# Small software scratch, a third staging and a fourth split buffer for weights, and other places and orders at the entrance of a channel mixer

## The chip, the cores and the metric

The kernel runs on one core of one Trainium2 chip. The metric is the device time of one execution in microseconds (us); the time before is the median of three runs. Engines: PE is TensorE, DVE VectorE, ACT ScalarE, POOL GpSimd, SP SyncE, which here issues all transfers.

## The reference

A two-layer encoder trunk over 512 tokens of width 1024 in float32:

```
for layer in range(2):
    hn = rms_norm(x, norm_mix_pre[layer])
    m  = retention_na_mixer(hn, ...) if layer == 0 else ssd_mixer(hn, ...)
    x  = x + rms_norm(m, norm_mix_post[layer])
    f  = conv_geglu_ffn(rms_norm(x, norm_ffn_pre[layer]), ...)
    x  = x + rms_norm(f, norm_ffn_post[layer])
```

The first mixer joins retention heads and two-dimensional neighbourhood attention. The second, a state-space mixer, projects to z, x, B, C and dt, convolves x, B and C over five tokens, scans in both directions in chunks of 128, adds a skip, gates with silu(z), normalises in four groups and projects with w_out. The channel mixer is

```
u = conv3(hn @ w_up) + b;  gate, val = split(u);  (gelu(gate) * val) @ w_down
```

with an inner width of 2816 (22 blocks of 128).

## The kernel before

Each float32 operand of a large product is split into a high part (rounded to the matmul's format) and a low part (the rest), and each product is three matmuls: high by high, high by low, low by high (`mm3`, L83 to L88). `split` (L79 to L82) makes a pair: ScalarE copies the high part, VectorE subtracts to get the low part.

Weights come in units of 512 KB. `wunit` (L55) loads one into a staging tile `wst`, of which there are 2, and splits it into `whi` and `wlo`, of which there are 3 each; or, with `parts`, into four tiles of half the width given by the caller. These weight splits have a raised priority of 60. The activations lie in `xh` and `xl`, eight blocks of 128 features by 512 tokens.

`norm(t)` makes the normalised tile `xs` of 128 tokens; `turn(t)` (L134) transposes it with eight small matmuls into `pt` and splits that into `xh` and `xl` without a raised priority. `post_norm` (L168) adds a sublayer's normalised output to x, read from tiles `mg`.

The order of instructions on every engine, the queues of transfers included, is set by a planner: it walks a simulated time with a cost model, takes among the instructions that are ready the one that stands first in the program (a raised priority moves it ahead by that many instructions), and gives tiles their slots. It then puts in the waits. Every engine runs its list in order. Tiles come from pools. The pools of a stage are stacked behind those of the whole kernel; when a stage ends, the next one's pools come to lie on the same bytes, and they have to wait for the users of what lay there.

The second token mixer, `mixer1`, ends with group 3 of its heads: projections t6 and t7 with Silu into tiles `z` (L689, L692), `head` (decay matrices `e`, `ds` from rows `pb` that are broadcast from DRAM, L736), `inter` (`pi`, `ti`), `pair` (`py`, `y`, `yh`, `yl`). Its last output weights are four units: two in `whi` and `wlo`, two in memory that group 3 no longer needs (tiles `wo`). Then, for four tiles of 128 tokens and two halves of the width, `out_tile` makes `m` from the product and the sum of the other groups, which is kept in x (L828). Since x itself had been saved to DRAM as `xd`, it is loaded back at once (L829, on SyncE's queue); a square of `m`, the scaled tile `mg`, `post_norm` and `norm` follow.

`ffn` (L214) is the channel mixer. Its pool `ffn_h` holds 22 tiles `hh` and 22 `hl`; a second pool of it, `ffn_c`, holds the conv weights `cwt`, whose transfer is the first that `ffn` issues. Its first four units (up-projection, two blocks of gate and value) are loaded ahead: the first and second go to `whi` and `wlo`, the third and fourth to two `hh` and two `hl` each. Their products are made first for tokens 0 to 255 (column half c = 0), with the turns of token tiles 2 and 3 in between (`E.flush()`), then for tokens 256 to 511 (c = 1). Then come the convolutions and blocks 2 to 21, and the down-projection, `down_tm`.

All of it is preceded by a reserved scratch at the start of each SBUF partition, by default of 16384 bytes, for transfers whose descriptors are made in software.

Of the kernel before, what the change touches and what calls it, by code (L numbers as in the profile page):

```python
# [7 lines left out]
F32 = mybir.dt.float32  # L8
R32 = mybir.dt.float32r
# [6 lines left out]
P = 128  # L16
S = 512
# [5 lines left out]
NF = FFN // P  # L23


class Env:


    def __init__(self, ctx, tc):
        self.tc, self.nc = tc, tc.nc  # L30
        nc = self.nc
        pool = lambda name, bufs, **kw: ctx.enter_context(tc.tile_pool(name=name, bufs=bufs, **kw))
        self.const = pool("const", 1)
        self.res = pool("res", 1)
        self.wst = pool("wst", 2)
        self.whi = pool("whi", 3)
        self.wlo = pool("wlo", 3)
        self.gain = pool("gain", 2)
        self.tmp = pool("tmp", 7)
        self.small = pool("small", 6)  # L40
        pool("pad", 1).tile([P, 32], F32, name="pad")
        self.mm = pool("mm", 4, space=PSUM)
        self.px = pool("px", 4, space=PSUM)
        self.dram = pool("dram", 1, space=DRAM)


        head = self.const.tile([P, 96 + P], F32, name="head")
        self.ident, self.mhalf = head[:, 96:], head[:, 0:1]
        make_identity(nc, self.ident)
        nc.vector.memset(self.mhalf, -0.5)  # L50
        self.x = self.res.tile([P, NT, D], F32, name="x")
        self.xh = self.res.tile([P, KD, S], R32, name="xh")
        self.xl = self.res.tile([P, KD, S], R32, name="xl")
        self.late, self.xs = [], {}
# [79 lines left out]
    def turn(self, t):  # L134

        nc = self.nc
        for h, xs in enumerate(self.xs[t]):
            pt = self.px.tile([P, 4, P], F32, name="pt", tag="px")
            for j in range(4):
                nc.tensor.transpose(pt[:, j], xs[:, j * P:(j + 1) * P], self.ident)  # L140
            o = (slice(None), slice(h * 4, h * 4 + 4), slice(t * P, (t + 1) * P))
            self.split(self.xh[o], self.xl[o], pt)

    def post_half(self, st, t, n, ps, g_post, eng=None, m=None):

# [38 lines left out]
def down_tm(E, batches, w_dram, act, g_post, done, extra):  # L184

    st, ps = {}, {}
    nk = w_dram.shape[1] * 2
    k0 = [0, 0]  # L190
    for b, parts in enumerate(batches):
        last = b == len(batches) - 1
        ws = [(n, k0[n] + 2 * i, w_dram[n, k0[n] // 2 + i]) for n, u in parts for i in range(u)]
        ws = [(n, k, E.wunit(w, extra(i) if last else None)) for i, (n, k, w) in enumerate(ws)]
        for n, u in parts:
            k0[n] += 2 * u
        for t in range(NT):
            tt = slice(t * P, (t + 1) * P)
            for n, k1, w in ws:
                if k1 == 0:  # L200
                    late = len(ps) >= NT and last and len(parts) > 1 and t == 0
                    ps[n, t] = (E.px if late else E.mm).tile([P, 512], F32, name="mm", tag="px" if late else "mm")
                for i in range(2):
                    ah, al = act(k1 + i)
                    E.mm3(ps[n, t], ah[:, tt], al[:, tt], *w[i], k1 + i == 0, k1 + i == nk - 1)
                if k1 + 2 == nk:
                    E.post_half(st, t, n, ps[n, t], g_post)
            if last:
                E.finish(DOWN[t], st, done)
    E.late += [lambda s=s: E.finish(s, st, done) for s in LATE]  # L210


def ffn(E, w_up, cw, w_down, g_post_row, done):

    nc, tc = E.nc, E.tc
    with ExitStack() as ctx:
        hp = ctx.enter_context(tc.tile_pool(name="ffn_h", bufs=NF))
        cp = ctx.enter_context(tc.tile_pool(name="ffn_c", bufs=1))
        cwt = cp.tile([P, 2, NF, 4], F32, name="cwt")
        nc.sync.dma_start(cwt, cw)  # L220
        hs = []

        def conv(ps, s, f):
            w = lambda i: cwt[:, s, f, i:i + 1]
            o = E.tmp.tile([P, S], F32, name=f"cv{s}", tag="tmp")
            nc.scalar.activation(o, ps, AF.Identity, scale=w(1), bias=w(3))  # L226
            nc.vector.scalar_tensor_tensor(o[:, 1:], ps[:, :S - 1], w(0), o[:, 1:], op0=ALU.mult, op1=ALU.add)  # L227
            nc.vector.scalar_tensor_tensor(o[:, :S - 1], ps[:, 1:], w(2), o[:, :S - 1], op0=ALU.mult, op1=ALU.add)  # L228
            return o

        def tail(f, pg, pv):
            g = conv(pg, 0, f)
            nc.scalar.activation(g, g, AF.Gelu_apprx_tanh)  # L233
            v = conv(pv, 1, f)
            nc.vector.tensor_tensor(v, g, v, op=ALU.mult)  # L235
            h = (hp.tile([P, S], R32, name="hh"), hp.tile([P, S], R32, name="hl"))
            E.split(*h, v)
            hs.append(h)

        extra = lambda i=0: [hp.tile([P, S], R32, name=n) for n in ("hh", "hh", "hl", "hl")]  # L240
        w0 = [[E.wunit(w_up[s, f], extra() if 2 * f + s >= 2 else None) for s in range(2)] for f in range(2)]
        p0 = [[E.mm.tile([P, S], F32, name="mm") for s in range(2)] for f in range(2)]
        for c in range(2):
            for i in range(4):
                f, s = i // 2, i % 2
                E.proj_fm(p0[f][s], w0[f][s], c * 256, c * 256 + 256)
                if c == 0 and i in (1, 2):
                    E.flush()
        for f in range(2):
            tail(f, *p0[f])  # L250
        for f in range(2, NF):
            ps = []
            for s in range(2):
                w = E.wunit(w_up[s, f])
                ps.append(E.mm.tile([P, S], F32, name="mm"))
                E.proj_fm(ps[-1], w)
            tail(f, *ps)
        g_post = E.bcast(g_post_row)
        batches = [[(0, u)] for u in (2, 2, 2, 2, 2, 1)] + [[(1, u)] for u in (2, 2, 1, 6)]
        down_tm(E, batches, w_down, lambda k: hs[k], g_post, done, lambda i: extra() if i not in (2, 3) else None)  # L260
# [292 lines left out]
def mixer1(E, w_dt, w_fm, cw, dtc, cols, mask, w_out, g_post_row, done):  # L553
# [4 lines left out]
    nc, tc = E.nc, E.tc  # L558
    C = P
    H, H2 = SSD_H, 2 * SSD_H  # L560
    with ExitStack() as ctx:
        pool = lambda name, bufs: ctx.enter_context(tc.tile_pool(name=name, bufs=bufs))
# [5 lines left out]
        cwt = few.tile([P, NG, 6, 6], F32, name="cwt")  # L568
# [7 lines left out]
        xd = E.dram.tile([NT, P, D], F32, name="xd")  # L576
# [231 lines left out]
        def out_mm(o, t, ws):  # L808
            ps = E.mm.tile([P, 512], F32, name="mm")
            tt = slice(t * P, (t + 1) * P)  # L810
            for k in range(4):
                yh, yl = o["y"][k]
                E.mm3(ps, yh[:, tt], yl[:, tt], *ws[k], k == 0, k == 3)
            return ps

        def out_tile(o, n, t, ws, fin=None, ps=None):
            g = o["g"]
            ns = slice(n * 512, n * 512 + 512)
            if ps is None:
                ps = out_mm(o, t, ws)  # L820
            acc, r = E.x[:, t, ns], o["r"][:, t:t + 1]
            if g == 0:
                nc.scalar.activation(acc, ps, AF.Identity, scale=r)
            elif g < NG - 1:
                nc.vector.scalar_tensor_tensor(acc, ps, r, acc, op0=ALU.mult, op1=ALU.add)
            else:
                m = three.tile([P, 512], F32, name="m", tag="e")
                nc.vector.scalar_tensor_tensor(m, ps, r, acc, op0=ALU.mult, op1=ALU.add)  # L828
                nc.sync.dma_start(acc, xd[t, :, ns])  # L829
                fin(t, n, m)  # L830

        def out(o, n):
            ws = E.wunit(w_out[o["g"], n, 0]) + E.wunit(w_out[o["g"], n, 1])
            for t in range(NT):
                out_tile(o, n, t, ws)
# [7 lines left out]
        w0 = [E.wunit(w_fm[0, i]) for i in range(3)]  # L843
# [12 lines left out]
        for g, o in enumerate(gs):  # L856
            nx = gs[g + 1] if g + 1 < NG else None
            for step in SLOTS[g].split():
                a, i = step[0], int(step[1:] or 0)
# [24 lines left out]
        def fin(t, n, m):  # L884
            E.post_half(st, t, n, m, g_post, None, four.tile([P, 512], F32, name="mg", tag="z"))
# [14 lines left out]
def trunk(tc, x, norms, ab, ssd, ffns, out):  # L900

    nc = tc.nc
    with ExitStack() as ctx:
# [26 lines left out]

        mixer0(E, w0, *ab, norms[0, 1], then(norms[0, 2]))
        ffn(E, *ffns[0], norms[0, 3], then(norms[1, 0]))
        mixer1(E, *ssd, norms[1, 1], then(norms[1, 2]))
        ffn(E, *ffns[1], norms[1, 3], store)
        while E.late:
            E.flush()
# [106 lines left out]
```

## Time and profile before

| | |
|---|---|
| median of three runs | 1433.8 us (1433.73 to 1433.99) |
| the profiled execution, its own time | 1435.78 us |
| its span, first to last instruction | 1434.0 us |
| mean granted TensorE clock | 0.996 of full speed |
| TensorE, VectorE, ScalarE, GpSimd busy | 98%, 66%, 50%, 4% |
| transfers | 166.34 MB, mean 116 GB/s, all on one hardware queue |
| stages | mixer0 to 255 us, channel mixer to 660, mixer1 to 1058, channel mixer to the end |

In a timeline, each row is one or several like instructions: start, length, engine, line, operation, output <- inputs, their shape and count, and in brackets how long the engine was idle before them and what ended that. `issue` in such a bracket means that the profile shows nothing that the engine waited for. `SPq` is SyncE's queue.

### The profile page before, as it was taken

What the parts mean: (1) busy time and instruction counts of PE and PEld (TensorE: products, weight loads), DVE (VectorE), ACT (ScalarE), POOL (GpSimd) and SP (SyncE); (2) the same over time, 40 slices, a digit from 0 to 9 for tenths busy, and PEclk for the clock granted to TensorE, in tenths of its full rate; (3) what the DMA queues carried; (4) which work ended last, traced back from release to release, by engine and by line L of the source; (5) the groups of instructions that cost most, each with busy time, mean ns of one, the idle gap of its engine ahead of it and who ended that gap; (6) DMA issues with size and microseconds to landing.
All of it is one profiled execution on the core that took longest, in us unless ns stands there. A gap on an engine that the chain in (4) does not pass through costs nothing.

```text
span 1434.0 us, 18009 instructions
## 1 busy us (share of the span) xinstructions
PE 1398.5 (98%) x6832; PEld 1141.0 (80%) x6832; DVE 946.3 (66%) x1486; ACT 720.3 (50%) x1192; POOL 60.6 (4%) x67
## 2 busy tenths in 40 slices
PE   7999999999999999999999999999889999999998
PEld 6877777898888888888777787777678888888886
DVE  7368888666566552357889786999886666564242
ACT  5356665454444431334888766577544444443230
POOL 0010110100000000000000000000110000000000
PEclk9999999999999999999999999999999999999999
DMA  7443232233233333332556354345432233333241
GB/s 255 146 141 92 85 96 77 83 108 102 89 98 95 102 94 97 120 107 95 159 180 184 111 176 131 95 153 162 143 120 87 90 100 94 100 89 102 89 132 59
DMA packets 56950, 166.34 MB, mean 116 GB/s; under 512 B 7200, under 2 KB 7968, under 8 KB 56864
## 3 DMA queue, kind: packets, MB, share of 16 engines
q1 hardware_dynamic: 56864, 165.20, 37.2%
q8 instruction: 54, 0.88, 0.2%
q14 instruction: 32, 0.26, 0.1%
HBM read 157.57 MB, written 5.51 MB: 114 GB/s over the span
## 4 chain that ended last, share of the span: by engine, by line
PE 80%; DVE 9%; ACT 5%; DMA 3%; issue 2%; POOL 0%; SPq 0%; DVEq 0%; POOLq 0%; ACTq 0%
PE mm L86 24%; PE mm L87 24%; PE mm L88 24%; DMA pb<-pd 1%; DVE wlo L82 1%; PE st L719 1%; DVE xf L683 1%; PE pt L140 1%; PE y L449 1%; PE pi L762 1%; DMA wst<-in_c_out 1%; PE pt L663 1%; PE py L782 1%; DVE ti L766 1%; DVE yl L795 0%
## 5 line engine op out<-in xcount | busy, mean ns | idle before, releaser
L88 PE MATMUL mm<-xl,whi 128*128 128x512 f32 (+2 forms) x1216 | 463.9, 382 | 4.0 <-DVE xl L82 3.8
L86 PE MATMUL mm<-xh,whi 128*128 128x512 f32 (+2 forms) x1216 | 464.0, 382 | 1.5 <-ACT z L689 0.7
L87 PE MATMUL mm<-xh,wlo 128*128 128x512 f32 (+2 forms) x1216 | 463.4, 381 | 1.4 <-DVE wlo L82 1.4
L82 DVE TENSOR_TENSOR wlo<-wst,whi 128x1024 fp32r<-128x1024 f32 (+1 forms) x208 | 255.5, 1229 | 198.0 <-ACT whi L81 195.8
L81 ACT CAST whi<-wst 128x1024 fp32r<-128x1024 f32 (+1 forms) x208 | 217.3, 1045 | 191.4 <-PE mm L87 119.6
L88 PEld LDWEIGHTS mm<-xl,whi 128*128 128x128 f32 (+1 forms) x1216 | 228.6, 188 | 48.4 <-DVE xl L82 4.5
L86 PEld LDWEIGHTS mm<-xh,whi 128*128 128x128 f32 (+1 forms) x1216 | 229.0, 188 | 46.8 <-issue 2.4
L87 PEld LDWEIGHTS mm<-xh,wlo 128*128 128x128 f32 (+1 forms) x1216 | 229.0, 188 | 45.2 <-DVE wlo L82 2.7
L227 DVE SCALAR_TENSOR_TENSOR cv<-mm,cwt,cv 128x511 f32<-128x511 f32 x88 | 65.7, 747 | 95.2 <-ACT cv L226 94.9
L86 PE MATMUL mm<-whi,hh 128*128 128x512 f32 x288 | 112.0, 389 | 0.0
L87 PE MATMUL mm<-whi,hl 128*128 128x512 f32 x288 | 112.0, 389 | 0.0
L88 PE MATMUL mm<-wlo,hh 128*128 128x512 f32 x288 | 112.0, 389 | 0.0
L226 ACT ACTIVATE cv<-mm,cwt 128x512 f32<-128x512 f32 x88 | 68.4, 777 | 39.8 <-PE mm L88 39.8
L81 ACT CAST hh<-cv 128x512 fp32r<-128x512 f32 x44 | 27.3, 621 | 100.5 <-DVE cv L235 100.3
L233 ACT ACTIVATE cv<-cv 128x512 f32<-128x512 f32 x44 | 27.8, 633 | 85.2 <-DVE cv L228 85.2
L228 DVE SCALAR_TENSOR_TENSOR cv<-mm,cwt,cv 128x511 f32<-128x511 f32 x88 | 66.0, 750 | 3.0
L744 ACT ACTIVATE ds<-um,tok,ddt 128x128 f32<-128x128 f32 x128 | 55.7, 484 | 16.1 <-DVE e L747 15.7
L88 PEld LDWEIGHTS mm<-wlo,hh 128*128 128x128 f32 x288 | 54.1, 188 | 11.3
L87 PEld LDWEIGHTS mm<-whi,hl 128*128 128x128 f32 x288 | 54.1, 188 | 11.2
L86 PEld LDWEIGHTS mm<-whi,hh 128*128 128x128 f32 x288 | 54.1, 188 | 11.2
L82 DVE TENSOR_TENSOR hl<-cv,hh 128x512 fp32r<-128x512 f32 x44 | 30.5, 693 | 28.9 <-ACT hh L81 28.9
L741 ACT ACTIVATE e<-pb,tok 128x128 f32<-128x128 f32 x128 | 43.0, 392 | 11.7 <-DMA pb<-pd 10.2
(236 smaller groups left out, 1945.6 us busy)
## 6 DMA issues: line engine op xcount, KB each, us to landing
wst<-in_f_up SPq DMA_DIRECT2D x88, 512.0 KB
wst<-in_f_down SPq DMA_DIRECT2D x44, 512.0 KB
wst<-in_c_fm SPq DMA_DIRECT2D x40, 512.0 KB
pb<-pd SPq DMA_DIRECT2D x64, 256.0 KB
wst<-in_ab_fm SPq DMA_DIRECT2D x20, 512.0 KB
gain<-yd SPq DMA_DIRECT2D x32, 256.0 KB
wst<-in_c_out SPq DMA_DIRECT2D x16, 512.0 KB
gain<-in_norms SPq DMA_DIRECT2D x8, 512.0 KB
```

Of the source, the lines that this page charges most:

```text
L81: self.nc.scalar.copy(hi, src)
L82: self.nc.vector.tensor_tensor(lo, src, hi.bitcast(F32), op=ALU.subtract)
L86: mm(out, lh, rh, start=first, stop=False)
L87: mm(out, ll, rh, start=False, stop=False)
L88: mm(out, lh, rl, start=False, stop=last)
L140: nc.tensor.transpose(pt[:, j], xs[:, j * P:(j + 1) * P], self.ident)
L226: nc.scalar.activation(o, ps, AF.Identity, scale=w(1), bias=w(3))
L227: nc.vector.scalar_tensor_tensor(o[:, 1:], ps[:, :S - 1], w(0), o[:, 1:], op0=ALU.mult, op1=ALU.add)
L228: nc.vector.scalar_tensor_tensor(o[:, :S - 1], ps[:, 1:], w(2), o[:, :S - 1], op0=ALU.mult, op1=ALU.add)
L233: nc.scalar.activation(g, g, AF.Gelu_apprx_tanh)
L741: nc.scalar.activation(e[:, c], pb[0][:, cc], AF.Identity, scale=-1.0, bias=tok[:, 0, c, h:h + 1])
L744: nc.scalar.activation(ds[:, c], um, AF.Identity, scale=ddt[:, c, h:h + 1], bias=tok[:, 1, c, H + h:H + h + 1])
```

## The change

The software scratch shrinks from 16384 to 1024 bytes per partition. `wst` gets 3 buffers, `whi` and `wlo` 4 each. The conv weights `cwt` of the channel mixers move from a pool of `ffn` to the pool of constants, beside a pad of 320 bytes, and their transfer is issued after those of the first four units. The fourth unit's parts are three tiles `hh` and one `hl`. In `turn`, the split gets a raised priority of 100. The reload of x at the end of mixer1 is issued by ScalarE.

```diff
-        self.wst = pool("wst", 2)
-        self.whi = pool("whi", 3)
-        self.wlo = pool("wlo", 3)
+        self.wst = pool("wst", 3)
+        self.whi = pool("whi", 4)
+        self.wlo = pool("wlo", 4)
...
+        self.cwt = self.const.tile([P, 2, NF, 4], F32, name="cwt")
+        self.const.tile([P, 80], F32, name="pad")
...
-            self.split(self.xh[o], self.xl[o], pt)
+            with self.tc.high_priority(100):
+                self.split(self.xh[o], self.xl[o], pt)
...
-        cp = ctx.enter_context(tc.tile_pool(name="ffn_c", bufs=1))
-        cwt = cp.tile([P, 2, NF, 4], F32, name="cwt")
-        nc.sync.dma_start(cwt, cw)
+        cwt = E.cwt
...
-        extra = lambda i=0: [hp.tile([P, S], R32, name=n) for n in ("hh", "hh", "hl", "hl")]
-        w0 = [[E.wunit(w_up[s, f], extra() if 2 * f + s >= 2 else None) for s in range(2)] for f in range(2)]
+        extra = lambda *names: [hp.tile([P, S], R32, name=n) for n in names or ("hh", "hh", "hl", "hl")]
+        own = None, None, extra(), extra("hh", "hh", "hh", "hl")
+        w0 = [[E.wunit(w_up[s, f], own[2 * f + s]) for s in range(2)] for f in range(2)]
+        nc.sync.dma_start(cwt, cw)
...
-                nc.sync.dma_start(acc, xd[t, :, ns])
+                nc.scalar.dma_start(acc, xd[t, :, ns])
...
-    nc = bacc.Bacc("TRN2", target_bir_lowering=False, num_devices=1)
+    nc = bacc.Bacc("TRN2", target_bir_lowering=False, num_devices=1, dynamic_dma_scratch_size=1024)
```

## Rows read from the trace of the kernel before

**Rows 1.** The page: busy time by engine, and TensorE's busy tenths in 40 slices.
```profile
PE 1398.5 (98%) x6832; PEld 1141.0 (80%) x6832; DVE 946.3 (66%) x1486; ACT 720.3 (50%) x1192; POOL 60.6 (4%) x67
...
PE   7999999999999999999999999999889999999998
```

**Rows 2.** Busy time by stage: window, length, PE, PEld, DVE, ACT, POOL, clock, DMA.
```profile
700.00:1020.00 320.00, 315.15 (x1636) 251.40 (x1635) 279.98 (x491) 233.29 (x457) 16.46 (x12) 1.00 0.51 152
1020.00:1082.00 62.00, 50.76 (x305) 42.46 (x304) 49.34 (x79) 28.93 (x55) 10.44 (x12) 0.94 0.38 122
```

**Rows 3.** TensorE's waits from 1018 to 1080 us: total, times, longest.
```profile
PE py L782 <- DVE ti L766: 4.1, 2, 3.7
PE mm L88 <- DVE xl L82: 3.8, 1, 3.8
```

**Rows 4.** The chain that ended last, in the passage: start, length, what.
```profile
1016.57 4.42 DMA wst<-in_c_out
...
1065.69 0.61 DVE xl L82
```

**Rows 5.** Timeline of ScalarE, the kernel's start and the passage.
```profile
0.73 1.28 ACT L119 ACT_TABLE_LOAD   x1 [0.73 <-PEq L1033]
...
1021.01 1.14 ACT L81 CAST wo<-wst 128x512 fp32r<-128x512 f32 x2 [1.39 <-DMA wst<-in_c_out]
1022.17 1.28 ACT L689 ACT_TABLE_LOAD   x1
...
1068.63 2.18 ACT L81 CAST hh<-wst 128x512 fp32r<-128x512 f32 x4 [4.58 <-issue]
```

**Rows 6.** Timeline of VectorE in the passage.
```profile
1021.66 1.90 DVE L82 TENSOR_TENSOR wo<-wst,wo 128x512 fp32r<-128x512 f32 x3 [1.83 <-ACT wo L81]
1024.10 0.69 DVE L786 TENSOR_TENSOR y<-y,z 128x512 f32<-128x512 f32 x1 [0.54 <-ACT z L689]
...
1058.18 1.22 DVE L82 TENSOR_TENSOR wlo<-wst,whi 128x1024 fp32r<-128x1024 f32 x1
...
1062.93 0.68 DVE L82 TENSOR_TENSOR xl<-pt,xh 128x512 fp32r<-128x512 f32 x1
...
1067.06 1.41 DVE L175 SCALAR_TENSOR_TENSOR x<-mg,r_m,x 128x512 f32<-128x512 f32 x2 [0.65 <-POOL r_m L111]
...
1072.71 1.41 DVE L131 SCALAR_TENSOR_TENSOR xs<-x,r_x,gain 128x512 f32<-128x512 f32 x2 [0.66 <-POOL r_x L111]
...
1076.51 1.28 DVE L82 TENSOR_TENSOR xl<-pt,xh 128x512 fp32r<-128x512 f32 x2
```

**Rows 7.** Timeline of TensorE in the passage.
```profile
1020.88 0.39 PE L88 MATMUL mm<-xl,whi 128*128 128x512 f32 x1
...
1059.50 0.34 PE L87 MATMUL mm<-xh,wlo 128*128 128x256 f32 x1
1063.67 0.39 PE L88 MATMUL mm<-xl,whi 128*128 128x256 f32 x1 [3.83 <-DVE xl L82]
...
1071.61 0.36 PE L86 MATMUL mm<-xh,hh 128*128 128x256 f32 x1
...
1078.30 0.28 PE L86 MATMUL mm<-xh,whi 128*128 128x256 f32 x1
```

**Rows 8.** Timeline of SyncE's queue in the passage.
```profile
1029.05 0.33 SPq L61 DMA_DIRECT2D wst<-in_f_up  x1
1043.84 9.86 SPq L829 DMA_DIRECT2D x<-xd  x6
```

**Rows 9.** Busy time in one stretch of 2 us: DMA share and GB/s last.
```profile
1032.00:1034.00 2.00, 2.00 (x10) 1.66 (x9) 2.00 (x6) 0.00 (x0) 0.00 (x0) 1.00 0.69 281
```

**Rows 10.** TensorE's waits from 690 to 1016 us, the first row.
```profile
PE mm L87 <- DVE wlo L82: 1.4, 2, 0.8
```

**Rows 11.** The chain that ended last, in the body of mixer1.
```profile
713.57 4.44 DMA pb<-pd
...
875.89 7.63 DMA pb<-pd
```

## The prediction

> **What bounds the kernel now.** I read the page first. TensorE is busy for 98% of the span, and its line of forty slices has one dip in the middle, in two slices of 35.85 us each that begin at 1004 us [rows 1]. The table by stage puts a size on it: from 1020 to 1082 us, the passage from the second token mixer (mixer1) into the second channel mixer, TensorE works 50.76 of 62 us; from 700 to 1020 us, the body of mixer1, it works 315.15 of 320 us [rows 2]. So 11.2 us are open in the passage and 4.85 us in the body; elsewhere TensorE has no gap that weights or buffers could fill, and its work there is not changed.
>
> The waits of TensorE in the passage name two stalls: a single wait of 3.7 us of py for ti, and one of 3.8 us of a projection for xl [rows 3]. The chain of waits says what stands behind each [rows 4]. Behind the first is a transfer: 4.42 us of wst<-in_c_out, the last output weights of mixer1. Behind the second is VectorE's order of work: xl, the low half of a transposed tile, comes late.
>
> In the first stall, ScalarE's copy of those weights at 1021.01 waited 1.39 us for their transfer, and its table load for Silu follows only at 1022.17 [rows 5]. VectorE therefore waits 1.83 us for wo and 0.54 us for z [rows 6]. In the second, TensorE starts the channel mixer at 1059, stops after the matmul at 1059.50, and goes on at 1063.67, after 3.83 us [rows 7]. VectorE did a weight's low half at 1058.18 and other work first, and only at 1062.93 this xl [rows 6].
>
> **Deeper weight buffers, end of mixer1.** With a third wst buffer and a fourth whi and wlo, a weight's load waits for the split of the third unit before it, not of the second. That takes the 4.42 us transfer off the chain. What is late next is TensorE itself: the last projection ends at 1020.88 + 0.39 = 1021.27 [rows 7], and Silu reads its result. The first table load of the kernel ran at 0.73, ahead of the data its activation needed [rows 5], so I let this one run early too, and Silu starts near 1021.35 instead of 1022.17 + 1.28 = 1023.45. Gain 2.1 us. It is 0.8 us if the table load stays behind a copy (1022.6 against 1023.45), and at most 2.4 us of VectorE idleness (1.83 + 0.54) can go. I take 2.1, since the data of the copies is then there before the projections end.
>
> **The fourth whi and wlo and the second weight of the channel mixer.** Its low half, 1.22 us on VectorE at 1058.18, stands in front of the stalled xl because its slot was held by mixer1's output weights. With four slots it runs before the run of m tiles. That takes 1.2 us out of the passage. If it lands in VectorE's full stretch before that, it is a loss of 1.2 us there and the net is 0; if the first unit's low half, equally long, also moves into idle time, the gain is 2.4 us. I take 1.2: the first unit leaves the full stretch as the second enters it.
>
> **Transposes' splits first.** The xl at 1062.93 then runs right after its xh, and the 3.83 us stall shrinks to about 0.7 us. This does not come out whole, because of what is late next: the third and fourth units. Their halves go into the channel mixer's own pool (hh, hl). The third unit's load was issued at 1029.05 [rows 8] and DMA traffic of 281 GB/s ended about 1034 [rows 9], yet its copy started only at 1068.63, after 4.58 us of idleness that the profile calls issue [rows 5]. VectorE's last read of a mixer1 tile, x<-mg of the fourth token tile, ended at 1067.06 + 1.41 = 1068.47 [rows 6], 0.16 us before. I read this as the whole pool waiting for the last reader of the pools beneath it. The change leaves the third and fourth unit in that pool and only takes one piece from hh instead of hl, so I expect the wait to stay.
>
> The end of the passage then follows from that x<-mg. Before: it ends at 1068.47, xs of the last tile starts at 1072.71, its xl ends at 1076.51 + 1.28 = 1077.79 (9.3 us later), and the second column half starts at 1078.30 [rows 6, 7]. After: x<-mg ends 2.1 + 1.2 = 3.3 us earlier, at 1065.2; the third unit's first copy (0.55 us, a quarter of the 2.18) and its low half (0.64, half of an xl pair) let TensorE go on at 1066.6 instead of 1071.61 [rows 5 to 7]. From there to the second half lie two units and one group of transposes, 1078.30 - 1071.61 = 6.7 us. The last xs ends at 1072.71 + 1.41 - 3.3 = 1070.8, while the third unit, 24 matmuls at 0.12 us, ends at 1069.5: 1.3 us of waiting. 1066.6 + 6.7 + 1.3 = 1074.6, and the last xl is there at 1065.2 + 9.3 = 1074.5. So the passage gains 3.7 us, limited by x<-mg and not by the 3.83 us stall. Bounds: 0.5 us (late table load, nothing for the second weight, 0.3 us lost to the new order) to 5.3 us (2.4 + 2.4, and 0.5 at the last xs).
>
> **Reload of x on ScalarE's queue.** Eight transfers x<-xd leave SyncE. Six of them took 9.86 us of SyncE's time between 1043.84 and 1053.7 while weights for the channel mixer were queued behind them [rows 8]. SyncE's rows give 0.33 us for one issue; no row has a transfer issued by ScalarE. Each waits for m, as the next instruction on ScalarE, a square of m, does anyway; behind them in its queue stand the squares whose sums make r_m, for which x<-mg waits. Two issues a tile lie on that path: 0.66 us, of which half is hidden while VectorE does other tiles. I take 0.3 us of loss; ends are 0 (issue during ScalarE's idle time) and 1.5 us (eight issues of 0.33 us, 2.6, less what VectorE's other work covers). The page "DMA: Bandwidth & Descriptors" of the Trainium skill, section "Issuing engines are not separate DMA queues", speaks against a gain in the transfer: whichever engine starts them, they run on the same 16 DMA engines and interleave, and only issue time is saved. By it a reload beside a weight now in flight would land later and this term would be 1.5 us and the time 1430.6; the trace before, where all are on SyncE, cannot show it.
>
> **Body of mixer1, 700 to 1020 us.** Of its 4.85 us, TensorE waits 1.4 us for low halves of weights (wlo), in two waits [rows 10]. Deeper buffers remove these; part comes back as waits for VectorE, so I take 1.0 us. Ends: 2.4 us gained (half the idle time) and 1 us lost by a new order of instructions, since deeper buffers move splits ahead of other work on ScalarE and VectorE.
>
> **At nothing.** The smaller scratch, the pads and the place of the conv weights: TensorE is full at the first use of cwt, 1082 us; if that cover were gone, one late transfer, of no more than the 4.42 us of a whole weight [rows 4], would be the price. Earlier turns and the first channel mixer: TensorE has no dip there [rows 1]. I allow 0.7 us either way.
>
> **Sum.** -3.7 + 0.3 - 1.0 = -4.4 us. The profiled execution took 1435.78 us (span 1434.0 and 1.78 around it), 1.98 us above the median of 1433.8. On it: 1431.4; on the median: **1429.4 us**.
>
> **Rivals.**
> *The memory does come free early* (1427.2 us). If each tile of the channel mixer waits only for its own bytes, the four copies and low halves leave the stretch after x<-mg, and the last square of x follows without 2.2 us of copies in front of it. Then 2.2 us more are gained. For it: no row shows which bytes the 1068.63 copy waited for. Against: all four copies run together right behind the last x<-mg.
>
> *Absorbed* (1433.3 us). VectorE is the limit from 1043 on and the deeper buffers only put splits earlier into its full stretches; the 0.5 us of the low bound is left. For it: VectorE has 49.34 busy of 62 us, with only 12.7 us free [rows 2]. Against: 2.4 us of that idleness lies just in front of its full stretch [rows 6].
>
> *Weights crowd out the decay rows in mixer1* (slower, 1436.6 us). Loads pb<-pd, one broadcast row per head and direction, stand on the chain with four pieces over 3.5 us, the first at 713.57 and the last, of 7.63 us, at 875.89 [rows 11]. If a third weight is issued ahead of each, it takes 512 KB / 281 GB/s = 1.8 us more [rows 9], 7.2 us in four: 1429.4 + 7.2. It decides as soon as SyncE issues a weight before a pb that ScalarE already waits for. For it: these waits are exposed now. Against: a SyncE that is not held by a full wst also reaches pb sooner.
>
> **Chances and range.** Forecast 0.52, memory free 0.15, absorbed 0.20, crowding 0.13. About 0.2% (2.9 us) is what a measurement tells from no change, so faster means under 1430.9. The forecast's own range is 1426.5 to 1433; about three quarters of it count as faster (0.40), the memory rival wholly (0.15): 0.55. Same: 0.12 + 0.18 = 0.30. Slower: crowding and a little of the rest, 0.15. The range that holds 8 in 10 reaches from 1425 (passage 5.3, body 2.4 and 1 us of the memory rival) to 1435 (nothing gained, 1.2 us lost), and leaves out most of the crowding.
>
> **What would show it.** Right: wo copies before 1020, Silu within 0.3 us of the last projection, no py wait over 2 us; the second unit's copy before the first m; xl directly behind xh; hh copies still behind the last x<-mg; the second column half 3 to 4 us earlier. Wrong: hh copies before that x<-mg (memory rival), pb pieces longer (crowding), or the same distance from the last m to the second column half (absorbed).

## The result, and the profile after

The changed kernel is slower: 1439.97 us (median of 6 runs, 1436.79 to 1445.01) against 1433.97 (6 runs), a ratio of 1.0042 with a 95% interval of 1.0030 to 1.0054, or 6.0 us. I had forecast 4.4 us less. The profiled execution took 1440.17 us with a span of 1438.4, so its span is 4.4 us longer than the one before. Ratios leave out two executions whose core was held at a lower clock throughout; one is e1's profiled execution (mean clock 0.849), so no row of e1 is read.

Three marks cut the span into stretches: the last projection matmul on TensorE, the first m on VectorE, and the end.

| stretch | before | after | difference | forecast |
|---|---|---|---|---|
| start to last projection | 1020.88 | 1022.03 | +1.15 | -1.0 |
| last projection to first m | 22.18 | 19.75 | -2.43 | -2.1 |
| first m to end | 390.94 | 396.62 | +5.68 | -1.3 |

(The -1.3 is the rest of the -4.4: 1.2 and 0.4 off the passage, 0.3 for the reload.) The first two stretches nearly cancel. The loss lies behind the first m.

Page and table by stage of the changed kernel, to be read with [rows 1, 2]: the dip has a deeper slice, the passage has 49.07 us of TensorE for 50.76, at a clock of 0.92 for 0.94, and the body 312.79 for 315.15.
```profile
PE   7999999999999999999999999999879999999998
```
```profile
700.00:1020.00 320.00, 312.79 (x1626) 250.18 (x1625) 278.04 (x491) 235.50 (x462) 16.57 (x12) 0.99 0.49 151
1020.00:1082.00 62.00, 49.07 (x272) 40.59 (x271) 49.17 (x79) 27.73 (x53) 11.72 (x12) 0.92 0.37 119
```
TensorE's waits from 1018 to 1080 us. The two of [rows 3] are gone or halved: no wait for xl, 1.8 us for ti. In their place stand waits for xs, hh and yl.
```profile
PE pt L143 <- DVE xs L134: 4.2, 2, 3.1
PE mm L89 <- ACT hh L84: 3.8, 1, 3.8
PE mm L90 <- DVE yl L799: 2.2, 2, 1.6
PE py L786 <- DVE ti L770: 2.1, 2, 1.8
```
VectorE from 1060 to 1072 us. Before, one low half of a weight stood here, at 1058.18 [rows 6], and v_m of the third tile ran at 1059.32, ahead of both xl (1062.93 and 1065.61):
```profile
1059.32 0.20 DVE L109 TENSOR_SCALAR v_m<-ssm,ssm 128x1 f32<-128x1 f32 x1
...
1060.17 1.41 DVE L175 SCALAR_TENSOR_TENSOR x<-mg,r_m,x 128x512 f32<-128x512 f32 x2
```
Now there are two low halves. The pair of xl runs ahead of v_m in the third tile, and between v_m and x<-mg in the fourth, whose x<-mg starts at 1070.54 for 1067.06.
```profile
1060.13 1.22 DVE L85 TENSOR_TENSOR wlo<-wst,whi 128x1024 fp32r<-128x1024 f32 x1
1061.26 1.28 DVE L85 TENSOR_TENSOR xl<-pt,xh 128x512 fp32r<-128x512 f32 x2
1062.46 0.20 DVE L112 TENSOR_SCALAR v_m<-ssm,ssm 128x1 f32<-128x1 f32 x1
1063.32 1.41 DVE L179 SCALAR_TENSOR_TENSOR x<-mg,r_m,x 128x512 f32<-128x512 f32 x2 [0.65 <-POOL r_m L114]
...
1068.09 1.22 DVE L85 TENSOR_TENSOR wlo<-wst,whi 128x1024 fp32r<-128x1024 f32 x1
1069.22 0.21 DVE L112 TENSOR_SCALAR v_m<-ssm,ssm 128x1 f32<-128x1 f32 x1
1069.35 1.28 DVE L85 TENSOR_TENSOR xl<-pt,xh 128x512 fp32r<-128x512 f32 x2
1070.54 1.41 DVE L179 SCALAR_TENSOR_TENSOR x<-mg,r_m,x 128x512 f32<-128x512 f32 x2
```
Measured from the first m, x<-mg of the four tiles starts after 3.43, 10.28, 17.11 and 24.00 us before, and after 5.09, 12.53, 21.54 and 28.76 us now. So 1.7 of the 4.8 us are there at the first tile, where no xl runs yet.

ScalarE. The table load runs ahead of its data and Silu (the z rows) starts 0.04 us after the last projection ends (1022.03 + 0.39). Later, the square of the second tile's m, which was ready at 1045.72 (VectorE's row at 1044.31, 1.41 long), stands behind x<-xd of the third tile, which waits for that tile's m: 1.25 us of idleness in front of it, and it starts at 1050.72. The hh copies still start behind the last x<-mg.
```profile
1020.20 1.28 ACT L693 ACT_TABLE_LOAD   x1
1022.46 0.60 ACT L693 ACTIVATE z<-mm 128x512 f32<-128x512 f32 x1 [0.98 <-PE mm L91]
...
1049.58 1.09 ACTq L833 DMA_DIRECT2D x<-xd  x2
1050.72 0.63 ACT L122 ACTIVATE junk<-m 128x512 bf16<-128x512 f32 x1 [1.25 <-DVE m L832]
...
1072.06 1.66 ACT L84 CAST hh<-wst 128x512 fp32r<-128x512 f32 x3 [2.49 <-DVE x L179]
```
The page "PSUM — Partial Sum Buffer" of the Trainium skill, section "Engine vs sequencer instructions", calls the queues of ScalarE and VectorE strict FIFO; the trace agrees, by a square that is ready and lets 1.25 us pass.

TensorE. After the hh wait it runs the third unit, 24 matmuls, in 5.8 us (1072.73 to 1078.53).
```profile
1072.73 0.58 PE L89 MATMUL mm<-xh,hh 128*128 128x256 f32 x1 [3.79 <-ACT hh L84]
...
1078.53 1.44 PE L143 MATMUL pt<-head,xs 128*128 128x128 f32 x8
```
In the table by stage the granted clock of this stretch (third number from the end) is 0.50, the lower of the two levels, 1.2 for 2.4 GHz:
```profile
1073.00:1079.00 6.00, 5.85 (x27) 5.56 (x28) 3.78 (x7) 2.28 (x5) 0.55 (x1) 0.50 0.45 135
```
In kernel g2 below, which does not wait for hh, the same 24 take 2.9 us (1068.56 to 1071.50) at full clock:
```profile
1068.00:1074.00 6.00, 6.00 (x54) 6.00 (x53) 5.34 (x10) 4.22 (x8) 0.54 (x1) 1.00 0.51 179
```
So the wait for hh is paid twice: 3.8 us of it and 2.9 us behind it. The xl stall of before had the lower clock behind it too, from about 1064 to 1068 us. In the changed kernel two stretches take its place, one behind the 3.1 us wait for xs (about 1059 to 1063) and a longer one behind hh (about 1072.5 to 1079.5). From 1056 to 1088 us, before and then after, the mean granted clock is 0.95 and 0.84:
```profile
1056.00:1088.00 32.00, 27.18 (x206) 25.76 (x205) 24.61 (x39) 16.42 (x31) 2.71 (x5) 0.95 0.36 119
```
```profile
1056.00:1088.00 32.00, 24.94 (x165) 23.62 (x166) 19.73 (x33) 14.10 (x27) 3.09 (x5) 0.84 0.31 100
```

### The profile page after: what moved, and what is told of

Same layout as the page of the kernel before. It is cut to its first block, busy times and chain, and to the rows that moved or that the text cites. A ratio compares the mean times of both kernels' runs of the same rounds, so it can differ in the third digit from the quotient of the medians.

```text
span 1438.4 us, 17989 instructions
## 1 busy us (share of the span) xinstructions
PE 1400.0 (97%) x6832; PEld 1143.0 (79%) x6832; DVE 943.7 (66%) x1486; ACT 718.8 (50%) x1192; POOL 61.1 (4%) x67
## 4 chain that ended last, share of the span: by engine, by line
PE 83%; DVE 6%; ACT 4%; DMA 3%; issue 2%; POOL 1%; SPq 0%; DVEq 0%; POOLq 0%; ACTq 0%
PE mm L89 25%; PE mm L90 25%; PE mm L91 25%; DMA pb<-pd 2%; PE pi L766 1%; PE st L723 1%; DVE wlo L85 1%; PE pt L143 1%; PE y L453 1%; ACT ds L748 1%; PE py L786 1%; ACT whi L84 1%; ACT e L745 1%; PE sc L437 1%; PE pt L667 0%
## 5 line engine op out<-in xcount | busy, mean ns | idle before, releaser
L89 PE MATMUL mm<-xh,whi 128*128 128x512 f32 (+1 forms) x1216 | 464.3, 382 | 1.0 <-DVE xf L687 0.7
L89 PEld LDWEIGHTS mm<-xh,whi 128*128 128x128 f32 x1216 | 228.6, 188 | 45.8 <-issue 2.5
L687 DVE SCALAR_TENSOR_TENSOR xf<-mm,cwt,xf 128x511 f32<-128x511 f32 (+1 forms) x64 | 47.2, 741 | 3.2 <-ACT xf L684 3.1
```

The lines of the kernel that those rows point to most:

```text
L89: mm(out, lh, rh, start=first, stop=False)
L687: nc.vector.scalar_tensor_tensor(r[:, a], ps[:, b], wc(j), r[:, a], op0=ALU.mult, op1=ALU.add)
```

## The experiments

All ratios are to the kernel before, timed beside each kernel on the same chip. Its median lay between 1434.0 and 1435.8 us there, so ratios are compared, not microseconds. 0.001 is 1.4 us. The last column is read from one profile each; the kernel before has 390.94 there.

| kernel | from | edits | ratio | 95% interval | first m to end |
|---|---|---|---|---|---|
| changed | before | all | 1.0042 | 1.0030, 1.0054 | 396.62 |
| e1 | changed | reload on SyncE | 1.0036 | 1.0023, 1.0049 | |
| e2 | changed | splits not first | 1.0011 | 1.0000, 1.0022 | 391.69 |
| e3 | changed | buffers 2, 3, 3 | 1.0021 | 1.0009, 1.0034 | 396.10 |
| e4 | changed | reload on SyncE, splits not first | 0.9993 | 0.9982, 1.0004 | 391.05 |
| f3 | before | splits first | 1.0017 | 1.0007, 1.0027 | 394.96 |
| g1 | before | pool by tile | 1.0000 | 0.9991, 1.0009 | 391.45 |
| g2 | e4 | pool by tile | 0.9984 | 0.9976, 0.9993 | 390.31 |
| g3 | e1 | pool by tile | 1.0025 | 1.0013, 1.0038 | 395.14 |
| n1 | f3 | post-norm ahead | 0.9991 | 0.9982, 1.0000 | 391.17 |
| n2 | g3 | post-norm ahead | 1.0015 | 1.0004, 1.0027 | 393.07 |
| n3 | g2 | post-norm ahead | 0.9991 | 0.9983, 1.0000 | 389.64 |
| k1 | g2 | 2 wst | 0.9994 | 0.9985, 1.0003 | 390.25 |
| a1 | changed | post-norm ahead | 1.0027 | 1.0014, 1.0040 | 394.19 |
| f2 | before | reload on ScalarE | 1.0003 | 0.9995, 1.0012 | 392.96 |
| n6 | n1 | pool by tile | 0.9987 | 0.9979, 0.9996 | 390.42 |
| w1 | g2 | pd and yd writes on ScalarE | 0.9991 | 0.9983, 1.0000 | 390.10 |

**One part undone at a time: e1 to e4.**
```diff
 e1, e4                                  e2, e4
-nc.scalar.dma_start(acc, xd[t, :, ns])  -with self.tc.high_priority(100):
+nc.sync.dma_start(acc, xd[t, :, ns])    -    self.split(self.xh[o], self.xl[o], pt)
 e3                                      +self.split(self.xh[o], self.xl[o], pt)
-wst 3, whi 4, wlo 4
+wst 2, whi 3, wlo 3
```


> The changed kernel with the reload x<-xd back on SyncE; all else as changed. Theory A (the reload on ScalarE stands in order ahead of the squares of the tile before it): the squares of token tile 1 follow their m within 2 us instead of 5 to 6.7 us, v_m of tile 1 comes about 1 us earlier, every x<-mg behind it too, and the time is 1438.5 against 1440.0. Theory B (the deeper buffers are the cause): x<-mg of the last tile moves by less than 0.5 us and the time stays at 1439.5 to 1440.5. Theory C (transposes' splits first are the cause): the same as B.

> The changed kernel with the transposes' splits at their old place in the order; all else as changed. Theory C (the two xl put ahead of v_m of tile 2 delay x<-mg of tiles 2 and 3): v_m of tile 2 runs ahead of the two xl, x<-mg of the last tile is 1.2 us earlier, and the 3.8 us stall of TensorE for xl of before comes back in part: 1438.8 to 1440. Theory A and B: no better than 1439.5, and with the xl stall back up to 1441.

> The changed kernel with 2 wst, 3 whi and 3 wlo as before; reload on ScalarE and splits first stay. Theory B (deeper buffers are the cause: two low halves of weights of 1.22 us ahead of xl and x<-mg in the passage, 2.4 us of TensorE idleness more in the body of mixer1, and 7 us more at half clock than before): 1433 to 1434.5, body busy 315 of 320 us again, and the stall of py for ti back at 3.7 us. Theories A and C: the passage stays late, 1437 to 1439.

> The changed kernel with the reload back on SyncE and the transposes' splits at their old place: what is left is the deeper buffers, the smaller scratch and the conv weights in the constants. Theory B: 1437.5 to 1440. Theories A and C together: 1431.5 to 1433.5, below the kernel before by the early Silu, since the end of mixer1 keeps its gain and x<-mg follows at the old distance.

e1 gained 0.0006, far inside its interval. e2 gained more than I had allowed to any part, 0.0031 or 4.4 us, with the xl stall back (3.1 us): splits first were worth less than nothing. e3 gained 0.0021 and kept the long passage, 396.10: the buffers don't make it long; its first m comes 2.3 us earlier (1039.50 for 1041.78). Theory B's time for e3, 1433 to 1434.5, was missed (1437.58). With both other edits undone, e4 is level with the kernel before. So C stands, and B falls as the main cause. A is unsettled: e1 puts the reload at 0.0006, while e2 and e4, which differ by it alone, lie 0.0018 (2.6 us) apart.

**Splits first alone, and the pool: f3, g1, g2, g3.**
```diff
 f3: turn(), as in the change            g1, g2, g3: ffn()
+with self.tc.high_priority(100):        -tc.tile_pool(name="ffn_h", bufs=NF)
+    self.split(self.xh[o], ...)         +tc.tile_pool(name="ffn_h", bufs=NF, reuse_waits="tile")
```


> The kernel before with one edit: the transposes' splits put first. Theory S (splits first lengthen the passage by themselves: on VectorE the two xl run ahead of v_m, and TensorE, no longer held in the middle of the first unit, runs dry in front of hh): first m to the first conv activation of the channel mixer 43 to 45 us instead of 39.3, a wait of TensorE for hh of 3 us or more, the wait for xl gone; the start of mixer1 1 us earlier; in all 1436 to 1438.5. Rival D (it hurts only with the second weight's split in the passage, which the deeper buffers bring): the distance stays at 39 to 40.5 us and the time is 1431.5 to 1434.

> The kernel before with one edit: each tile of the channel mixer's pool waits only for the earlier tiles on its own bytes, not for the whole pool. Theory P (the 1068.63 copy into hh waited for the pool's last reader, x<-mg of the fourth tile): the four hh copies run before that x<-mg ends. Gain small, since TensorE has no wait for hh in this kernel: 0 to 2 us, time 1433 to 1435. Rival: the copies are late for their place in ScalarE's order, and stay within 0.5 us of where they are.

> Deeper buffers, smaller scratch and conv weights in the constants, reload on SyncE, splits at their old place, and the pool of the channel mixer waiting tile by tile. Theory P: hh copies before the last x<-mg; with them out of ScalarE's way the last square of x and the last xs come 1 to 2 us earlier and the time is 1 to 2 us below the same kernel without it, 1432.5 to 1434. Rival (VectorE's order decides, hh is hidden): the same as without, 1434.5 to 1435.5.

> The changed kernel with the reload back on SyncE and the channel mixer's pool waiting tile by tile; splits first and deeper buffers stay. Theory S with P (what splits first cost is paid at the wait for hh, 3.8 us and the half clock behind it): that wait goes below 1 us, and the time falls by 3 to 6 us against the same kernel without tile by tile, to 1434.5 to 1437.5. Rival (the cost is VectorE's order, and x<-mg of tiles 2 and 3 is late whatever hh does): no more than 1.5 us gained, 1439 to 1441, with the wait moved to the last xs.

f3 is the plainest case: one line, 4.0 us more from the first m to the end, 2.4 us in the ratio. TensorE's waits from 1018 to 1080 us show what theory S said: the 3.8 us of xl are gone, and xs and hh take over.
```profile
PE pt L140 <- DVE xs L131: 3.4, 2, 2.4
PE mm L86 <- ACT hh L81: 3.2, 1, 3.2
```
VectorE in f3, second tile (first m at 1040.54): the pair xl runs before v_m, and x<-mg comes 11.73 us after the first m. Before it came after 10.28 us (1053.34 less 1043.06).
```profile
1050.22 1.28 DVE L82 TENSOR_TENSOR xl<-pt,xh 128x512 fp32r<-128x512 f32 x2
1051.41 0.20 DVE L109 TENSOR_SCALAR v_m<-ssm,ssm 128x1 f32<-128x1 f32 x1
...
1052.27 1.41 DVE L176 SCALAR_TENSOR_TENSOR x<-mg,r_m,x 128x512 f32<-128x512 f32 x2
```
g1 settles my memory rival's mechanism: with waits by tile the hh copies ran at 1062.09, before the last x<-mg (1065.19), so the pool's last reader did hold them. And it is worth nothing where TensorE does not wait for hh (1.0000). With deeper buffers (g2) the kernel is faster than before (0.9984); its 0.0009 over e4, the same kernel without it, is inside the intervals. ScalarE in g2: three copies before the last x<-mg, the fourth in the open.
```profile
1061.95 1.64 ACT L84 CAST hh<-wst 128x512 fp32r<-128x512 f32 x3
1067.47 1.06 ACT L122 ACTIVATE junk<-x 128x1024 bf16<-128x1024 f32 x1 [3.87 <-DVE x L178]
1068.43 0.19 ACT L122 ACTIVATION_READ_ACCUMULATOR junk<-x 128x1 f32 x1
1068.53 0.60 ACT L84 CAST hh<-wst 128x512 fp32r<-128x512 f32 x1
```
g3 gained 0.0011 on e1, the rival's size and inside the intervals: with splits first, x<-mg is late whatever hh does (29.0 us after the first m). But the wait did not move to the last xs, as the rival had it; TensorE still waits 2.1 us for hh and 2.0 for hl.

**Is it the place of v_m? n1, n2, n3, a1.**
```diff
 finish()
-    self.post_norm(st, t)
+    with self.tc.high_priority(200):
+        self.post_norm(st, t)
```


> The kernel before with two edits: splits first, and the post-norm (v_m, r_m, x<-mg) put ahead of them in the order. Theory V (splits first cost because the pair xl stands ahead of v_m on VectorE, tile after tile): x<-mg of the fourth tile is again within 24.5 us of the first m instead of 26.3 to 28.2, first m to first conv activation 39 to 41 us instead of 43.3, and the time 1433.5 to 1435.5 against 1437.7. Rival H (TensorE runs dry at hh and loses the half clock behind it, whatever VectorE's order): the distance stays above 42 us, 1436.5 to 1438.

> Deeper buffers, reload on SyncE, splits first, tile-by-tile pool, and the post-norm ahead of the splits. Theory V: the xl stall stays away and the last x<-mg comes 3 to 4 us earlier than without the last edit, first m to first conv activation 36 to 39 us instead of 42.5, the time 1431 to 1434 against 1439.3. Rival H: above 1436.

> As the kernel with deeper buffers, reload on SyncE, splits at their old place and tile-by-tile pool (1432.8), with the post-norm put ahead. Theory V has nothing to mend here, since v_m already runs ahead of xl: within 1.5 us of it, 1431.5 to 1434. Rival (the order of the whole passage matters more than the place of v_m): off by more than 2 us either way.

> The changed kernel with one edit more: the post-norm (v_m, r_m, x<-mg) put ahead of the transposes' splits. Theory V (the splits' place ahead of v_m is what the change lost by): x<-mg of the fourth tile within 26.5 us of the first m instead of 28.8, and 1435.5 to 1438, 2 to 4 us under the changed kernel's 1.0042 of before. Rival M (several small losses: reload on ScalarE, crowding at the start of mixer1, low halves of later weights in the passage, each 1 to 3 us and none undone by this): 1438.5 to 1440.

n1 takes f3's loss away: 0.9991 for 1.0017, 391.17 us for 394.96 (its last x<-mg comes 24.7 us after the first m, just over V's 24.5). The edit moves v_m and x<-mg together, so which of the two decides is not separated. VectorE in n1, second tile (first m at 1043.43): v_m, one xl, x<-mg after 10.56 us, the other xl.
```profile
1053.13 0.21 DVE L109 TENSOR_SCALAR v_m<-ssm,ssm 128x1 f32<-128x1 f32 x1
1053.25 0.68 DVE L82 TENSOR_TENSOR xl<-pt,xh 128x512 fp32r<-128x512 f32 x1
1053.99 1.42 DVE L177 SCALAR_TENSOR_TENSOR x<-mg,r_m,x 128x512 f32<-128x512 f32 x2
1055.32 0.69 DVE L82 TENSOR_TENSOR xl<-pt,xh 128x512 fp32r<-128x512 f32 x1
```
In n3, which had nothing to mend, the same edit is worth nothing (389.64 for 390.31, the ratio not better): theory V passes on both sides. On the changed kernel itself (a1) it gives back 0.0015, 2.2 us of 6.0, between V and rival M; the intervals overlap, so the time alone does not show it. In a1's trace x<-mg of the fourth tile starts 27.26 us after the first m for 28.76 (V wanted 26.5), and the wait for hh is 1.9 us for 3.8. n2 gained 0.0010, inside the intervals, and missed V's 1431 to 1434; its last x<-mg is early again (24.7 us after the first m for 29.0), but TensorE still waits 3.0 us for hh, now late in ScalarE's order. V explains f3 wholly and, by the trace, the changed kernel in part.

**The reload alone, and the best with old buffers: f2, n6.** f2 has the reload's line of the change, n6 is n1 with the pool by tile.

> The kernel before with one edit: the reload x<-xd issued by ScalarE. Theory A (two issues stand in ScalarE's order ahead of the squares, v_m of the first tile 1.3 us later): each x<-mg 1 to 1.6 us later after the first m, 1434 to 1436 (ratio 1.0003 to 1.0015). Rival (SyncE is freed and weights come earlier, ScalarE has the time): ratio 0.9985 to 1.0.

> The kernel before with splits first, the post-norm ahead of them, and the channel mixer's pool waiting tile by tile; buffers, scratch and reload as before. Theory V with P: no wait for xl over 1 us, the wait for hh (2.1 and 0.7 us without tile by tile) under 1 us, first m to first conv activation 38 to 39.5 us instead of 40.1, the time 1431.5 to 1433.5. Rival (the last xs is late anyway): 1433 to 1434.5, with the wait moved from hh to pt for xs.

f2's v_m of the first tile comes 3.85 us after the first m (1045.59 less 1041.74) for 2.53, and the passage is 2.0 us longer in its profile; the ratio says 0.4 us, interval -0.7 to 1.7. The delay is shown, its price in time is not (0.4 us here, 0.9 from e1, 2.6 between e2 and e4). By the page "DMA: Bandwidth & Descriptors" of the Trainium skill, section "Issuing engines are not separate DMA queues", only issue time could be saved by it; no run here shows a gain. n6 is faster than before too. Its longest wait for hh is 1.2 us for n1's 2.1, still over the 1 us expected; the 0.0004 it gained on n1 is inside the intervals.

**What the deeper buffers cost: k1, w1.**
```diff
 k1: Env.__init__              w1: steps(), also for yd<-ysc
-self.wst = pool("wst", 3)     -nc.sync.dma_start(pd[:, ...], pf[r])
+self.wst = pool("wst", 2)     +nc.scalar.dma_start(pd[:, ...], pf[r])
```


> As the kernel with deeper buffers, reload on SyncE, old splits and tile-by-tile pool (1432.8), but with 2 wst instead of 3; whi and wlo stay at 4. Theory W (the third wst lets SyncE issue two weights ahead of the writes pd<-pf at the start of mixer1, so that pb and e come 4 us late, TensorE waits 3.2 us at 722 and falls to half clock): that wait goes below 1 us, the last copy of x into mixer1 to the first gt falls from 57.5 to 56 us, no interval at half clock near 723; 1.5 to 4 us gained there, of which the 4.4 us transfer of the last output weights at the end of mixer1 takes back 0.4 to 2; in all 1430.5 to 1433. Rival (whi and wlo are what crowds): the wait stays and the time is 1433 to 1436.

> As the kernel with deeper buffers, reload on SyncE, old splits and tile-by-tile pool, with the four writes pd<-pf and yd<-ysc at the start of mixer1 issued by ScalarE in place of SyncE, where they stand behind three weights' loads that wait for a slot. Theory W: the first pd write goes out at 688 to 690 instead of 692.9, pb lands 2 to 4 us earlier, TensorE's wait for e at 722 (3.2 us) goes below 1 us and the half clock there goes; 1430 to 1432. Rival (pb itself stands behind the same weights on SyncE, and bandwidth sets when it lands): the wait stays over 2 us, 1432.5 to 1434.5.

Every profile with a third wst (e1's is not read) has a wait of about 3 us for e near 722 (but w1's), and in the table by stage a clock of 0.98 or 0.99 over 700 to 1020 us; the eight with two (k1 among them) have 1.00. The last projection starts at 1020.9 to 1026.4 us in the nine with three (mean 1023.5) and at 1017.5 to 1021.3 in the eight with two (mean 1019.2). So the +1.15 us of the one pair in the first table understates what is lost up to there. SyncE's queue in g2: three weights hold it until the first pd write at 692.91, from which pb follows.
```profile
680.66 12.12 SPq L64 DMA_DIRECT2D wst<-in_c_fm  x3
692.91 0.49 SPq L642 DMA_DIRECT2D pd<-pf  x1
...
699.54 1.41 SPq L739 DMA_DIRECT2D pb<-pd  x3
```
In k1, two weights, and all of it 2 us earlier.
```profile
680.01 10.70 SPq L64 DMA_DIRECT2D wst<-in_c_fm  x2
690.82 0.49 SPq L642 DMA_DIRECT2D pd<-pf  x1
...
697.25 1.41 SPq L739 DMA_DIRECT2D pb<-pd  x3
```
TensorE at py, g2 and then k1, and the clock of 718 to 728 us in the table by stage:
```profile
722.73 1.47 PE L785 MATMUL py<-e,xt 128*64 128x128 f32 x16 [3.21 <-DVE e L750]
```
```profile
721.28 1.09 PE L785 MATMUL py<-e,xt 128*64 128x128 f32 x16 [2.54 <-DVE e L750]
```
```profile
718.00:728.00 10.00, 6.79 (x41) 5.65 (x40) 9.19 (x17) 7.16 (x14) 0.00 (x0) 0.83 0.71 203
```
```profile
718.00:728.00 10.00, 7.41 (x50) 5.85 (x49) 8.90 (x18) 8.00 (x18) 0.00 (x0) 1.00 0.52 153
```
So the third wst does hold the decay rows back, by 2 us, but it is not the whole. k1 still waits for e, 2.54 us here and 0.7 us in two places behind, which is what its rival said of whi and wlo. In the kernel before, five weights are issued from 660 us, the last by 680.6, and the first pd write at 689.67 waits for none. k1 issues a sixth and g2 a seventh, and the write follows at once. From the save of x (xd<-x) to that write are 40.9 to 42.8 us in the seven profiles with 2, 3 and 3 buffers, 43.4 in k1 and 44.0 to 45.7 in the eight with three wst that issue it on SyncE.

k1 is no faster than g2 (0.9994 for 0.9984, intervals overlap): at the end of mixer1 it waits 3.1 us for yh, which on ScalarE stands behind a copy that waits for its load:
```profile
1031.23 1.04 ACT L84 CAST whi<-wst 128x1024 fp32r<-128x1024 f32 x1 [6.43 <-DMA wst<-in_f_up]
```
There the third wst gives something back: from the last projection to the first m g2 takes 19.77 us, k1 21.15. In w1 the pd write did not come earlier (692.90: on ScalarE it stood behind a weight's copy), and the wait for e fell to 0.5 us all the same; why is not settled. w1 gained nothing. That moving these writes helps is not shown.

## Why the prediction was wrong

- **Deeper buffers, end of mixer1: right.** Silu ran 0.04 us after the last projection, as stepped, and the stretch gained 2.43 us for 2.1.
- **Splits first and the second weight: the step that failed.** The prediction put x<-mg of the fourth tile at 1065.2, "2.1 + 1.2 = 3.3 us earlier", and let the new order cost 0.3 us at most, in a bound. It ended at 1071.95, 3.5 us late, and 4.8 us late counted from the first m. I counted where xl would run and never what it would be put ahead of: from the second tile on, xl (1.28 us a pair) stands ahead of v_m or of x<-mg, and the next square, xs and pt hang on these. f3 shows it alone (+4.0 us from the first m to the end, 2.4 us in the time), n1 takes it away. The first 1.7 of the 4.8 us are not its work: f2, with the reload alone, has the same x<-mg of the first tile, 5.09 us after the first m for 3.43. The wlo of the second unit did leave the passage (1026.56), but two others took its place, at 1060.13 and 1068.09: with more slots the next units' splits come in early. That these two cost time was not tried by itself.
- **The memory's wait: right**, and g1 shows its cause. But its price was wrong: I let TensorE go on at 1066.6; with xl out of the way it ran dry at 1068.95, waited 3.79 us for hh, and did the third unit at 1.2 GHz, 2.9 us more. No term of the sum priced the clock, neither what the old stalls cost by it nor what the new ones would.
- **The reload: right in its mechanism**, too small in the trace (1.3 us at the first v_m for 0.3 in all), not settled in the time.
- **Body: wrong in sign.** The waits for low halves went (none in the trace after), but 1.15 us were lost where 1.0 was to be gained, and about 4 in the mean of the profiles. The crowding rival came nearest, pb behind weights, but looked at the wrong place: most of the price is at the start of mixer1, not at the four pieces of [rows 11]. (Its 1.8 us for a weight should be 1.9: 524288 bytes at 281 GB/s.)
- **At nothing: not tried alone, and no cost shows.** e3 has the scratch, the pads and the places beside splits first and the reload; it stands at 1.0021, and f3 and f2 together at 1.0020.
- **Signs and rivals.** Six of the seven signs of being right came true; only the second column half did not, 4.4 us later (1082.68 for 1078.30) instead of 3 to 4 earlier. The six say what would move and none what it would push back. No rival had splits first as a cost.
- **What stays open.** With splits first, deeper buffers cost 0.0021 (the changed kernel against e3), and with the edits beside them 0.0028 (n2 against n6); without splits first, they gain 0.0016 (g2 against g1). Some of it lies ahead of the passage (first m at 1044.43 for 1040.58, clock 0.98 for 1.00 in the body), but one profile each does not settle why the two edits hurt each other.

## What to carry to other kernels

An edit of priority moves no work away: name every instruction that the raised one passes, and who waits for it. Where an engine in order carries both the feed of a stalled engine and the chain that releases the next tile, raise the chain's short instructions first; v_m is 0.2 us here, and moving it ahead with its x<-mg decided 3.8. Undo each part alone before judging a bundle: the deeper buffers, level alone, lost 3 to 4 us beside splits first.

## What was not expected of the hardware

Behind several TensorE stalls stood a stretch at the lower clock: in the changed kernel 24 matmuls behind the 3.8 us wait for hh took twice their time, and in the kernel before both stalls of [rows 3] had one. The length of a stall did not tell whether it came. In front of the same matmuls (py near 722 us, waiting for e) a stall of 2.80 us in g3 had one behind it, and a stall of 2.86 us in the changed kernel had none; from 718 to 728 us the granted clock is 0.83 in g3 and 1.00 in the changed kernel:
```profile
718.00:728.00 10.00, 7.20 (x42) 5.99 (x41) 8.83 (x15) 7.80 (x16) 0.00 (x0) 0.83 0.62 177
```
```profile
718.00:728.00 10.00, 7.14 (x50) 5.81 (x49) 10.00 (x18) 8.05 (x17) 0.00 (x0) 1.00 0.70 203
```
Behind a wait of only 1.54 us (for sq, 965.81) the changed kernel ran at 0.50 from 967 to 970 us. What decides it is not shown here. Executions of one program differ with the clock too: of the changed kernel's six, 1445.01 us goes with a mean clock of 0.990 and 1436.79 us with 0.995.
